# Compressed probabilities of two heads stacked on 128 rows, and one product for the bias rows of all heads

## The chip, the cores and the metric

The kernel runs on one core of a Trainium2 chip, as one launch. The metric is the device time of a run in microseconds (us). Everything is computed in 32-bit floats. TensorE is called PE in the profile, and its weight loads PEld; VectorE is DVE, ScalarE is ACT, GpSimd is POOL, and SP is the engine whose queue issues every DMA.

## What is computed

The reference is one decoder layer over 1024 tokens of width 2048: a projection `proj = h @ w_in` into 76 tiles of 128 channels, attention of 16 heads (4 groups of 4 heads, 64 channels a head), a state-space layer, gates, two branch products, an output product and a norm. Two pieces of it matter here. Scores get a bias that depends on the distance of query and key alone, through a table of 32 buckets; and each head attends, in one of three branches, to 63 compressed keys:

```python
def head_bias(dist):
    b = tbl[_t5_bucket(dist)]
    return jnp.moveaxis(b, -1, 0).reshape(G, R, *dist.shape)
...
s = jnp.einsum('bgrqd,bgnd->bgrqn', qs, kc).astype(jnp.float32)
s = s + head_bias(t[:, None] - cmp_end[None, :])
p_c = _masked_softmax(s, cmp_end[None, :] <= t[:, None])
o_c = jnp.einsum('bgrqn,bgnd->bgrqd', p_c.astype(dtype), vc)
...
o = o_c * g[..., 0:1] + o_s * g[..., 1:2] + o_w * g[..., 2:3]
```

## The kernel before, in words

**Products.** A product of accuracy near 32 bits is made of three passes of a faster type: the operand and the weights are each split into a high and a low part (`hi` by a copy on ACT, `lo` by a subtraction on DVE), and high times high, high times low and low times high are added in PSUM. `mm6` (L119 to L128) does so for the projection: 128 rows of weights, 512 tokens, six products for each of 16 slices of the 2048 channels. `dense` (L238) runs one projection tile: four units of weights of 256 KB, 24 products a unit, and a side job after each unit. `w_unit` (L104) loads a unit into one of two raw buffers and splits it into one of three pairs of buffers. Four more uses of the same scheme are the branch and output products (L454 to L464, L599 to L603).

**Order of the work.** The program is written stage by stage: the modulation (L147 to L205), the projection tiles with the state-space blocks between them (L403 to L418), the compressed keys and values (`compress`, L659), then the projection tiles of the gates with 22 early units of attention between them (L427 to L439), then 10 late units of attention with the branch products between them (L553 to L573), then the output. A scheduler that simulates the program places each engine's instructions within that, and each engine and the SP queue then runs its own list in order.

**Bias rows.** Between the modulation and the first `dense`, L336 to L351 make a table for each head. `rb` (32 buckets by 16 heads) is repeated 128 times a head into `rbx` (L345). For each head a plain 32-bit product of 32 rows (L348) gives the 384 biases by distance in all 128 partitions alike, in a PSUM bank from `bank()`; DVE adds a mask (L350, buffer `ln`), and SP stores 128 x 384 elements (192 KB) into `tz_d` in memory (L351). `bf_d` takes the mask itself, loaded as `mk` and stored again (L342, L343). Each group of attention later reads `tz_d` so that each partition is shifted by one element, as `BN` (L780).

**A unit of attention** (`Attention.unit`, L818) is one group of 4 heads and one block of 128 queries. PE makes the scores (L814), DVE adds the bias and takes the minimum, ACT takes the exponential. The probabilities lie with queries in the partitions, so `flip` (L931) transposes them on PE (L935), at most four pieces of 128 columns into one bank, and ACT and DVE split the bank into high and low (L939, L940). `values` (L954) multiplies them with the values into the unit's PSUM bank `O`, 128 partitions by 512 columns: the value tile has the high part of 64 channels and the low part of the same 64 channels side by side, so both come out above each other, and the end of the unit adds them (L1024 to L1027). For window and selected keys a piece is 128 keys by two heads, thus 128 rows and 256 columns (`weigh`, L962). For the compressed keys a head has 64 keys: `compressed_values` (L997) transposes each head's 128 x 64 block into 64 rows, and makes two products of 64 rows by 512 columns, one with the high and one with the low probabilities. `VC` (L781) is the value tile for that, 64 x 128, loaded once a group in each of the two attention stages.

Of the kernel before, what the change touches and what calls it, by code (L numbers as in the profile page):

```python
# [5 lines left out]
F32 = mybir.dt.float32  # L6
F32R = mybir.dt.float32r
# [6 lines left out]
ADD, SUB, MUL, MAX, MIN = ALU.add, ALU.subtract, ALU.mult, ALU.max, ALU.min  # L14
# [4 lines left out]
H = 16  # L19
# [31 lines left out]
def _hybrid(es, tc, A, out):  # L51
    nc = tc.nc
    V, S, P, PE = nc.vector, nc.scalar, nc.gpsimd, nc.tensor
    ld, st_ = nc.sync.dma_start, nc.sync.dma_start
    rd = nc.sync.dma_start
# [6 lines left out]
    def scratch(name, shape):  # L62
        return dp.tile(shape, F32, name=name)
# [15 lines left out]
    kcc_d = scratch("kcc_d", [128, G, 64])  # L79
    vcc_d = scratch("vcc_d", [64, G, 128])  # L80
    tz_d = [scratch(f"tz_d{g}", [4, 128, 384]) for g in range(G)]
    bf_d = scratch("bf_d", [128, 512])
    ob_d = [[scratch(f"ob_d{hf}_{i}", [2, 128, 512]) for i in range(8)] for hf in range(2)]
    oa_d = [[scratch(f"oa_d{hf}_{g}", [2, 128, 2, 512]) for g in range(G)] for hf in range(2)]
# [69 lines left out]
    for b in range(NB):  # L154
        t = xh.tile([128, T], F32, name=f"xa{b}", tag="xh"), xh.tile([128, T], F32, name=f"xb{b}", tag="xh")
# [25 lines left out]
    for k in range(0, KT, 2):  # L181
        mp = pp.tile([128, 512], F32, name="mp", tag="mp", bufs=2)
        for n in range(8):
            wa = was.pop(4 * k + n) if 4 * k + n in was else load_wa(4 * k + n)
            for i in range(2):
                r = 32 * (2 * n % 4 + i)
# [61 lines left out]
    def bank():  # L248
        return pss.tile([128, 512], F32, name="sps", tag="s")
# [86 lines left out]
    with tc.tile_pool(name="t5", bufs=1) as t5:  # L336
        rb = t5.tile([32, H], F32, name="rb")
        ld(rb, A["rel_bias"])
        oh = t5.tile([32, 384], F32, name="oh")
        ld(oh, A["onehot"][:, 384:])  # L340
        mk = t5.tile([128, 768], F32, name="mk")
        ld(mk, A["dist_mask"][0:1, :].to_broadcast([128, 768]))  # L342
        st_(bf_d, mk[:, :512])  # L343
        rbx = t5.tile([32, H, 128], F32, name="rbx")
        V.tensor_copy(rbx, rb.unsqueeze(2).to_broadcast([32, H, 128]))  # L345
        for h in range(H):
            tp = bank()
            PE.matmul(tp[:, :384], rbx[:, h], oh, start=True, stop=True)  # L348
            ln = t5.tile([128, 384], F32, name="ln", tag="ln", bufs=2)
            V.tensor_tensor(ln, tp[:, :384], mk[:, 384:], op=ADD)  # L350
            st_(tz_d[h // 4][h % 4], ln)  # L351

    def gate_steps():

# [51 lines left out]
    n = 0  # L406
# [332 lines left out]
class Attention:  # L739
# [25 lines left out]
    def group(self, g):  # L765
        V, rd, NK = self.nc.vector, self.rd, self.NK
        self.g = g

        def f(ap):
            return ap.bitcast(F32)  # L770


        if self.first == 0:
            self.window_keys(0, NK)
        self.KS = self.tl("ks", [128, NK], F32R, "k")
        rd(f(self.KS), self.k_d[0][g].rearrange("i d t -> (i d) t")[:, :NK])

        self.BN = self.tl("bn", [128, 4, 256], F32, "kv")
        t = self.tz_d[g]
        rd(self.BN, bass.AP(tensor=t.tensor, offset=t.offset + 127, ap=[[383, 128], [384 * 128, 4], [1, 256]]))  # L780
        self.VC = self.tl("vc", [64, 128], F32R, "kv")  # L781
        rd(f(self.VC), self.vcc_d[:, g])
        if self.BF is None:
            self.BF = self.tl("bf", [128, 384])
            t = self.bf_d
            rd(self.BF, bass.AP(tensor=t.tensor, offset=t.offset + 127, ap=[[511, 128], [1, 384]]))
        nb = NK // 128
        self.VS = self.tl("vs", [128, nb, 128], F32R, "kv")
        self.VW = self.tl("vw", [128, nb, 128], F32R, "kv")
        for v, t in ((self.VW, self.v_d[1][g]), (self.VS, self.v_d[0][g])):  # L790
            for hf in range(2):
                c = slice(4 * hf, min(4 * hf + 4, nb))
                rd(f(v)[:, c], t[hf][:, :c.stop - c.start])
        self.BC = self.tl("bc", [128, 4, 120 - 8 * self.first], F32, "kv")
        V.memset(self.BC[:, :, 0:48], 0.0)
        V.memset(self.BC[:, :, 63:], NEG)
        V.tensor_copy(self.BC[:, :, 48:63], self.BN[:, :, 31:256:16])
# [20 lines left out]
    def unit(self, qb):  # L818
# [4 lines left out]
        def f(ap):  # L823
            return ap.bitcast(F32)
# [106 lines left out]
        def flip(srcs, n):  # L931

            tp = self.psum("t")
            for i, x in enumerate(srcs):
                PE.transpose(tp[0:n, 128 * i:128 * i + 128], x, self.ident[:, :128])  # L935
            w = 128 * len(srcs)
            hi = self.tl("pth", [128, 512], F32R, "pt")
            lo = self.tl("ptl", [128, 512], F32R, "pt")
            S.copy(hi[0:n, :w], tp[0:n, :w])  # L939
            V.tensor_tensor(lo[0:n, :w], tp[0:n, :w], f(hi[0:n, :w]), op=SUB)  # L940
            return hi, lo
# [7 lines left out]
                compressed(h, ps[:, 64 * h:64 * h + 64])  # L949
        gt = self.gts[:, qb, 12 * g:12 * g + 12].rearrange("p (h c) -> p h c", c=3)  # L950
        nbw, nbs = nw // 128, ns // 128
        left = [2 * (nbw + nbs) + 1]

        def values(o, v, hl):  # L954
            left[0] -= 1
            for i, x in enumerate(hl):
                PE.matmul(o, v, x, start=O_new[0], stop=left[0] == 0 and i == 1)  # L957
                O_new[0] = False
# [36 lines left out]
            return r  # L995

        def compressed_values():  # L997
            values(O, self.VC, [x[0:64] for x in flip([pc[:, h] for h in range(4)], 64)])

        win = (2, window, pw, nbw, self.VW[:, qb + 1 - nbw:])  # L1000
        sel = (1, selected, pS, nbs, self.VS)
# [431 lines left out]
```

## Time and profile before

| | before |
|---|---|
| time, median of 3 runs | 3239.2 us (3238.16 to 3239.89) |
| time of the profiled execution | 3234.84 us |
| its span, first to last instruction | 3233.1 us |
| PE busy | 3162.2 us, 15603 matrix instructions |
| DVE busy | 1686.2 us |
| ACT busy | 1127.2 us |
| mean granted clock of TensorE | 0.991 |
| read from and written to memory | 331.30 MB and 98.05 MB |

The times in the rows come from the profiled execution, which took 4.4 us less than the median. "Busy" of PE is time in which a matrix instruction is in its pipeline; since they overlap, what one costs is seen from the distance of the starts, not from its own duration. The granted clock is a share of the higher of two levels, 1.2 and 2.4 GHz.

### The profile page before, as it was taken

What the parts mean: (1) busy time and instruction counts of PE and PEld (TensorE: products, weight loads), DVE (VectorE), ACT (ScalarE), POOL (GpSimd) and SP (SyncE); (2) the same over time, 40 slices, a digit from 0 to 9 for tenths busy, and PEclk for the clock granted to TensorE, in tenths of its full rate; (3) what the DMA queues carried; (4) which work ended last, traced back from release to release, by engine and by line L of the source; (5) the groups of instructions that cost most, each with busy time, mean ns of one, the idle gap of its engine ahead of it and who ended that gap; (6) DMA issues with size and microseconds to landing.
All of it is one profiled execution on the core that took longest, in us unless ns stands there. A gap on an engine that the chain in (4) does not pass through costs nothing.

```text
span 3233.1 us, 43112 instructions
## 1 busy us (share of the span) xinstructions
PE 3162.2 (98%) x15603; PEld 2538.1 (79%) x15603; DVE 1686.2 (52%) x4615; ACT 1127.2 (35%) x2327; POOL 85.5 (3%) x66
## 2 busy tenths in 40 slices
PE   7999999999999999999999999999999999999896
PEld 4467788888888888888888888887888888788784
DVE  8354678763444434334333334426777665534737
ACT  4212222222433334333433234325555443322323
POOL 0000000000000000000000000000000000000302
PEclk9999999999999999999999999999999999999998
DMA  9654524344322232222322222236668444734533
GB/s 335 236 170 147 172 94 141 103 128 119 117 92 74 77 97 88 71 64 83 97 77 74 67 84 91 76 126 202 213 207 285 142 131 147 241 114 144 166 119 138
DMA packets 286398, 432.21 MB, mean 134 GB/s; under 512 B 40324, under 2 KB 139428, under 8 KB 286184
## 3 DMA queue, kind: packets, MB, share of 16 engines
q1 hardware_dynamic: 286184, 429.45, 41.0%
q8 instruction: 123, 2.02, 0.3%
q14 instruction: 91, 0.75, 0.1%
HBM read 331.30 MB, written 98.05 MB: 133 GB/s over the span
## 4 chain that ended last, share of the span: by engine, by line
PE 93%; DVE 3%; DMA 2%; ACT 1%; issue 1%; SPq 0%; ACTq 0%; DVEq 0%
PE dps L124 17%; PE dps L125 17%; PE dps L128 17%; PE po L957 5%; PE ps L814 4%; PE pt L935 4%; PE pa L462 4%; PE pa L463 4%; PE pa L464 4%; PE e L602 2%; PE e L601 2%; PE e L603 2%; PE mp L187 2%; DVE r L595 1%; PE acc L124 1%; PE e L462 1%
## 5 line engine op out<-in xcount | busy, mean ns | idle before, releaser
L124 PE MATMUL dps<-hhi,whi 128*128 128x512 f32 x2336 | 927.8, 397 | 0.0
L125 PE MATMUL dps<-hlo,whi 128*128 128x512 f32 x2336 | 925.2, 396 | 0.0
L128 PE MATMUL dps<-hhi,wlo 128*128 128x512 f32 x2336 | 750.3, 396 | 0.0
L111 ACT CAST whi<-wraw 128x512 fp32r<-128x512 f32 x544 | 336.2, 619 | 1054.9 <-PE dps L125 622.7
L113 DVE TENSOR_TENSOR wlo<-wraw,whi 128x512 fp32r<-128x512 f32 x544 | 381.0, 701 | 600.9 <-ACT whi L111 587.8
L124 PEld LDWEIGHTS dps<-hhi,whi 128*128 128x128 f32 x2336 | 439.7, 188 | 103.8 <-issue 13.0
L125 PEld LDWEIGHTS dps<-hlo,whi 128*128 128x128 f32 x2336 | 439.8, 188 | 93.7 <-issue 7.0
L128 PEld LDWEIGHTS dps<-hhi,wlo 128*128 128x128 f32 x2336 | 433.4, 188 | 92.5 <-issue 5.7
L940 DVE TENSOR_TENSOR ptl<-pt,pth 128x512 fp32r<-128x512 f32 (+2 forms) x320 | 204.1, 646 | 269.3 <-ACT pth L939 267.6
L939 ACT CAST pth<-pt 128x512 fp32r<-128x512 f32 (+2 forms) x320 | 172.0, 552 | 456.7 <-PE pt L935 456.0
L462 PE MATMUL pa<-op,whi 128*128 128x512 f32 x528 | 210.0, 400 | 2.1 <-ACT op L449 1.7
L463 PE MATMUL pa<-op,whi 128*128 128x512 f32 x528 | 209.7, 397 | 2.5 <-DMA op<-oa_d 2.5
L464 PE MATMUL pa<-op,wlo 128*128 128x512 f32 x528 | 208.8, 396 | 0.0
L602 PE MATMUL e<-wlo,m 128*128 128x512 f32 x368 | 148.0, 402 | 9.9 <-DVE rsd L42 5.4
L603 PE MATMUL e<-whi,m 128*128 128x512 f32 x368 | 146.3, 398 | 0.0
L929 ACT ACTIVATE psl<-psl,mn 128x128 f32<-128x128 f32 (+7 forms) x128 | 99.2, 775 | 81.3 <-DVE mn L842 80.5
L601 PE MATMUL e<-whi,m 128*128 128x512 f32 x368 | 122.0, 401 | 0.6 <-ACT whi L111 0.6
L462 PEld LDWEIGHTS pa<-op,whi 128*128 128x128 f32 x528 | 99.8, 189 | 23.3 <-ACT op L449 3.3
L463 PEld LDWEIGHTS pa<-op,whi 128*128 128x128 f32 x528 | 99.6, 189 | 22.9 <-DMA op<-oa_d 2.9
L464 PEld LDWEIGHTS pa<-op,wlo 128*128 128x128 f32 x528 | 99.6, 189 | 20.1 <-issue 0.7
L904 POOL TENSOR_TENSOR near<-bn,msk 128x512 f32<-128x512 f32 x32 | 35.1, 1098 | 2662.1 <-DVE msk L900 2535.9
L883 ACT ACTIVATE pw<-pw,mn 128x640 f32<-128x640 f32 (+4 forms) x128 | 88.9, 694 | 32.4 <-DVE mn L842 31.6
(308 smaller groups left out, 4271.1 us busy)
## 6 DMA issues: line engine op xcount, KB each, us to landing
wraw<-in_w_in SPq DMA_DIRECT2D x304, 256.0 KB, 3.0
wraw<-in_w_out SPq DMA_DIRECT2D x136, 256.0 KB, 3.0
wa<-in_w_ss SPq DMA_DIRECT2D x64, 512.0 KB, 5.7
wg<-in_w_gate SPq DMA_DIRECT2D x32, 512.0 KB, 3.6
q<-q_d SPq DMA_DIRECT2D x64, 256.0 KB, 4.1
wraw<-in_w_bn SPq DMA_DIRECT2D x64, 256.0 KB, 3.1
q_d<-stg SPq DMA_DIRECT2D x32, 256.0 KB, 3.9
oa_d<-ptl SPq DMA_DIRECT2D x64, 128.0 KB, 2.2
```

Of the source, the lines that this page charges most:

```text
L111: S.copy(hi, raw)
L113: V.tensor_tensor(lo, raw, f(hi), op=SUB)
L124: PE.matmul(ps[hf], hi[:, ku], hhi[k][:, c], start=a, stop=False)
L125: PE.matmul(ps[hf], hi[:, ku], hlo[k][:, c], start=False, stop=False)
L128: PE.matmul(ps[hf], lo[:, ku], hhi[k][:, c], start=False, stop=z)
L462: PE.matmul(ps, hi[:, j], x[k][0], start=k == 0, stop=False)
L463: PE.matmul(ps, hi[:, j], x[k][1], start=False, stop=False)
L464: PE.matmul(ps, lo[:, j], x[k][0], start=False, stop=k == 7)
L601: PE.matmul(a, mk[0][:, t], hi, start=k == 0, stop=False)
L602: PE.matmul(a, mk[0][:, t], lo, start=False, stop=False)
L603: PE.matmul(a, mk[1][:, t], hi, start=False, stop=k == KT - 1)
L940: V.tensor_tensor(lo[0:n, :w], tp[0:n, :w], f(hi[0:n, :w]), op=SUB)
```

## The change

**Bias rows.** `rb` itself is the stationary operand, so one product of 32 rows gives the biases of all 16 heads in 16 partitions. DVE adds the mask once, SP stores the 16 rows in `t5_d` in memory, and sixteen DMAs then copy from memory to memory: one row of 384 elements, read 128 times, becomes the 128 x 384 table of a head in `tz_d`. `bf_d` is filled from the input in the same manner.

**Compressed values.** Two heads of a pair are transposed together, 128 x 128, so the even head lies in rows 0 to 63 and the odd head in rows 64 to 127. `VC` becomes two tiles of 128 x 128: for the even head the values stand in the upper 64 rows and zeros in the lower, for the odd head the other way round. Each parity is one product of 128 rows by 256 columns (the two pairs), high and low: four products a unit, into the columns of `O` of that parity. The zeros are set by DVE and the values loaded twice a group.

```diff
@@ -79,6 +79,7 @@
     kcc_d = scratch("kcc_d", [128, G, 64])
     vcc_d = scratch("vcc_d", [64, G, 128])
     tz_d = [scratch(f"tz_d{g}", [4, 128, 384]) for g in range(G)]
+    t5_d = scratch("t5_d", [H, 384])
     bf_d = scratch("bf_d", [128, 512])
     ob_d = [[scratch(f"ob_d{hf}_{i}", [2, 128, 512]) for i in range(8)] for hf in range(2)]
     oa_d = [[scratch(f"oa_d{hf}_{g}", [2, 128, 2, 512]) for g in range(G)] for hf in range(2)]
@@ -338,17 +339,17 @@
         ld(rb, A["rel_bias"])
         oh = t5.tile([32, 384], F32, name="oh")
         ld(oh, A["onehot"][:, 384:])
-        mk = t5.tile([128, 768], F32, name="mk")
-        ld(mk, A["dist_mask"][0:1, :].to_broadcast([128, 768]))
-        st_(bf_d, mk[:, :512])
-        rbx = t5.tile([32, H, 128], F32, name="rbx")
-        V.tensor_copy(rbx, rb.unsqueeze(2).to_broadcast([32, H, 128]))
+        mk = t5.tile([H, 384], F32, name="mk")
+        ld(mk, A["dist_mask"][0:1, 384:].to_broadcast([H, 384]))
+        tp = bank()
+        PE.matmul(tp[0:H, :384], rb, oh, start=True, stop=True)
+        ln = t5.tile([H, 384], F32, name="ln")
+        V.tensor_tensor(ln, tp[0:H, :384], mk, op=ADD)
+        st_(t5_d, ln)
+
         for h in range(H):
-            tp = bank()
-            PE.matmul(tp[:, :384], rbx[:, h], oh, start=True, stop=True)
-            ln = t5.tile([128, 384], F32, name="ln", tag="ln", bufs=2)
-            V.tensor_tensor(ln, tp[:, :384], mk[:, 384:], op=ADD)
-            st_(tz_d[h // 4][h % 4], ln)
+            st_(tz_d[h // 4][h % 4], t5_d[h:h + 1].to_broadcast([128, 384]))
+        st_(bf_d, A["dist_mask"][0:1, :512].to_broadcast([128, 512]))
 
     def gate_steps():
 
@@ -778,8 +779,11 @@
         self.BN = self.tl("bn", [128, 4, 256], F32, "kv")
         t = self.tz_d[g]
         rd(self.BN, bass.AP(tensor=t.tensor, offset=t.offset + 127, ap=[[383, 128], [384 * 128, 4], [1, 256]]))
-        self.VC = self.tl("vc", [64, 128], F32R, "kv")
-        rd(f(self.VC), self.vcc_d[:, g])
+
+        self.VC = self.tl("vc", [128, 2, 128], F32R, "kv")
+        for e in range(2):
+            V.memset(f(self.VC)[64 - 64 * e:128 - 64 * e, e], 0.0)
+            rd(f(self.VC)[64 * e:64 * e + 64, e], self.vcc_d[:, g])
         if self.BF is None:
             self.BF = self.tl("bf", [128, 384])
             t = self.bf_d
@@ -949,7 +953,7 @@
                 compressed(h, ps[:, 64 * h:64 * h + 64])
         gt = self.gts[:, qb, 12 * g:12 * g + 12].rearrange("p (h c) -> p h c", c=3)
         nbw, nbs = nw // 128, ns // 128
-        left = [2 * (nbw + nbs) + 1]
+        left = [2 * (nbw + nbs) + 2]
 
         def values(o, v, hl):
             left[0] -= 1
@@ -995,7 +999,11 @@
             return r
 
         def compressed_values():
-            values(O, self.VC, [x[0:64] for x in flip([pc[:, h] for h in range(4)], 64)])
+
+            hl = flip([pc[:, 2 * pr:2 * pr + 2].rearrange("p h n -> p (h n)") for pr in range(2)], 128)
+            Oe = O.rearrange("p (r e t) -> p r e t", r=2, e=2)
+            for e in range(2):
+                values(Oe[:, :, e], self.VC[:, e], [x[:, :256].rearrange("p (r t) -> p r t", r=2) for x in hl])
 
         win = (2, window, pw, nbw, self.VW[:, qb + 1 - nbw:])
         sel = (1, selected, pS, nbs, self.VS)
```

**Where it moves instructions.** The scheduler's order, one row an instruction or a run of alike ones; L numbers of the changed kernel are 1 higher as far as the bias rows (`mm6` is L120 to L129), and 4 to 8 higher further down (`flip` L939, `values` L961, scores L818).

PE, at the bias products (`sps<-oh,rbx`), a piece of the first `dense` in the kernel before; the first four stand in one row ahead of it, and six more follow it one at a time:

```order
L124 MATMUL dps<-hhi_1112,whi 128x512
L348 MATMUL sps<-oh,rbx 128x384 x2
L125 MATMUL dps<-hlo_1114,whi 128x512
L128 MATMUL dps<-hhi_1112,wlo 128x512 x2
L124 MATMUL dps<-hhi_1135,whi 128x512
L125 MATMUL dps<-hlo_1137,whi 128x512
L124 MATMUL dps<-hhi_1135,whi 128x512
L125 MATMUL dps<-hlo_1137,whi 128x512
L128 MATMUL dps<-hhi_1135,wlo 128x512
L348 MATMUL sps<-oh,rbx 128x384 x2
L128 MATMUL dps<-hhi_1135,wlo 128x512
```

PE, the same place in the changed kernel, from the last products of the stage ahead (`acc`):

```order
L126 MATMUL acc<-hlo_1414,whi 128x512 x2
L129 MATMUL acc<-hhi_1412,wlo 128x512 x2
L345 MATMUL sps<-oh,rb 16x384
L125 MATMUL dps<-hhi_1067,whi 128x512
L126 MATMUL dps<-hlo_1069,whi 128x512
L125 MATMUL dps<-hhi_1067,whi 128x512
L126 MATMUL dps<-hlo_1069,whi 128x512
L129 MATMUL dps<-hhi_1067,wlo 128x512 x2
```

All sixteen are one row now, and `dense` runs on behind it with no bias product between.

PE, the first unit's products with the compressed values (`po<-pth,vc` and `po<-ptl,vc`) among `dense`, before:

```order
L125 MATMUL dps<-hlo_1321,whi 128x512
L128 MATMUL dps<-hhi_1319,wlo 128x512 x2
L957 MATMUL po<-pth,vc 128x512
L814 MATMUL ps<-ks,q 128x256 x4
L957 MATMUL po<-ptl,vc 128x512
L124 MATMUL dps<-hhi_1342,whi 128x512
L125 MATMUL dps<-hlo_1344,whi 128x512
L124 MATMUL dps<-hhi_1342,whi 128x512
```

and in the changed kernel:

```order
L126 MATMUL dps<-hlo_1322,whi 128x512
L129 MATMUL dps<-hhi_1320,wlo 128x512 x2
L961 MATMUL po<-pth,vc 128x2x128
L818 MATMUL ps<-ks,q 128x256 x4
L961 MATMUL po<-ptl,vc 128x2x128
L961 MATMUL po<-pth,vc 128x2x128
L961 MATMUL po<-ptl,vc 128x2x128
L125 MATMUL dps<-hhi_1343,whi 128x512
L126 MATMUL dps<-hlo_1345,whi 128x512
L125 MATMUL dps<-hhi_1343,whi 128x512
```

Two products of 512 columns that stand apart became four of 2 x 128 columns, and three of them stand together. The transposes ahead of them (`pt<-ident,pc`) went from `64x128 x4` to `128x128 x2`.

SP, the stores of the bias tables (`tz_d<-ln`) among the loads of weights (`wraw`) and of the side job (`wg`), before:

```order
L109 DMA wraw<-in_w_in 128x512
L351 DMA tz_d_196<-ln 128x384 x2
L362 DMA wg<-in_w_gate 128x4x256 x2
L351 DMA tz_d_196<-ln 128x384 x2
L351 DMA tz_d_197<-ln 128x384 x4
L109 DMA wraw<-in_w_in 128x512
L351 DMA tz_d_198<-ln 128x384 x4
L109 DMA wraw<-in_w_in 128x512
L351 DMA tz_d_199<-ln 128x384 x4
```

and in the changed kernel, where `t_d` is `t5_d`:

```order
L110 DMA wraw<-in_w_in 128x512
L348 DMA t_d<-ln 16x384
L363 DMA wg<-in_w_gate 128x4x256 x2
L351 DMA tz_d_196<-t_d 128x384 x4
L110 DMA wraw<-in_w_in 128x512
L351 DMA tz_d_197<-t_d 128x384 x4
L351 DMA tz_d_198<-t_d 128x384 x4
L110 DMA wraw<-in_w_in 128x512
L351 DMA tz_d_199<-t_d 128x384 x4
L363 DMA wg<-in_w_gate 128x4x256
```

One small store stands ahead of the copies now, and the first load of weights behind it stands after four copies, the next after twelve.

## Rows read from the trace of the kernel before

**Rows 1.** The page: part 1 (busy), part 2 (rates), part 4 (chain by engine).

```profile
PE 3162.2 (98%) x15603; PEld 2538.1 (79%) x15603; DVE 1686.2 (52%) x4615; ACT 1127.2 (35%) x2327; POOL 85.5 (3%) x66
...
GB/s 335 236 170 147 172 94 141 103 128 119 117 92 74 77 97 88 71 64 83 97 77 74 67 84 91 76 126 202 213 207 285 142 131 147 241 114 144 166 119 138
...
PE 93%; DVE 3%; DMA 2%; ACT 1%; issue 1%; SPq 0%; ACTq 0%; DVEq 0%
```

**Rows 2.** Stretches: length; busy us PE, PEld, DVE, ACT, POOL; clock; DMA; GB/s.

```profile
200.00:250.00 50.00, 50.00 (x244) 34.01 (x245) 28.48 (x91) 7.22 (x13) 0.00 (x0) 1.00 0.49 156
...
2450.00:2500.00 50.00, 49.93 (x275) 42.26 (x274) 39.87 (x120) 28.67 (x60) 2.08 (x2) 1.00 0.96 334
```

**Rows 3.** Timeline of PE, one unit's compressed values: start us, us, instruction.

```profile
851.05 0.62 PE L128 MATMUL dps<-hhi,wlo 128*128 128x512 f32 x2
851.60 0.49 PE L957 MATMUL po<-pth,vc 64*128 64x512 f32 x1
852.02 0.74 PE L814 MATMUL ps<-ks,q 128*128 128x256 f32 x4
852.69 0.49 PE L957 MATMUL po<-ptl,vc 64*128 64x512 f32 x1
853.11 0.50 PE L124 MATMUL dps<-hhi,whi 128*128 128x512 f32 x1
853.45 0.39 PE L125 MATMUL dps<-hlo,whi 128*128 128x512 f32 x1
```

**Rows 4.** Instructions of L957: duration ns min/median/max, first and last start us, forms.

```profile
L957 PE MATMUL po<-pth,vc x32: 489/494/501, 851.6 to 2722.8; 64*128 64x512 f32 x32
```

**Rows 5.** The chain in order of time, late attention: start us, us.

```profile
2206.74 0.87 PE pt L935 x8
...
2236.99 0.84 PE po L957 x7
```

**Rows 6.** Timeline of PE round the bias products, 178 to 202 us.

```profile
178.82 4.03 PE L348 MATMUL sps<-oh,rbx 32*128 32x384 f32 x8 [1.86 <-ACT stg L214]
...
182.78 0.80 PE L124 MATMUL dps<-hhi,whi 128*128 128x512 f32 x1
...
187.20 0.62 PE L128 MATMUL dps<-hhi,wlo 128*128 128x512 f32 x2
...
188.12 0.40 PE L124 MATMUL dps<-hhi,whi 128*128 128x512 f32 x1
188.44 1.55 PE L348 MATMUL sps<-oh,rbx 32*128 32x384 f32 x4
189.92 0.50 PE L125 MATMUL dps<-hlo,whi 128*128 128x512 f32 x1
...
198.69 0.40 PE L124 MATMUL dps<-hhi,whi 128*128 128x512 f32 x1
199.02 0.91 PE L348 MATMUL sps<-oh,rbx 32*128 32x384 f32 x2
199.86 0.50 PE L125 MATMUL dps<-hlo,whi 128*128 128x512 f32 x1
200.29 0.91 PE L348 MATMUL sps<-oh,rbx 32*128 32x384 f32 x2
201.13 0.74 PE L128 MATMUL dps<-hhi,wlo 128*128 128x512 f32 x2
```

**Rows 7.** A stretch of 10 us at the bias products, columns as above.

```profile
180.00:190.00 10.00, 10.00 (x26) 5.92 (x24) 2.69 (x5) 0.58 (x1) 0.00 (x0) 0.66 1.07 333
```

**Rows 8.** Timeline of the SP queue: two loads of dense weights.

```profile
182.66 0.49 SPq L109 DMA_DIRECT2D wraw<-in_w_in  x1
...
197.07 0.33 SPq L109 DMA_DIRECT2D wraw<-in_w_in  x1
```

**Rows 9.** Instructions of L654: duration ns, first and last issue us; landing.

```profile
L654 SPq DMA_DIRECT2D gate<-gate_d x4: 650/788/877, 2752.6 to 2761.3; - x4
...
DMA to landing us min/median/max: 6.1/6.8/8.4
```

## Prediction

> **What bounds the kernel now.** I read the page first: PE is busy for 3162 of 3233 us, and PE makes 93% of the chain that ended last [rows 1]. Then the stretches of 50 us, to see whether that holds where the change acts. It does: at the bias products PE is busy for 50 of 50 us, and in the late attention for 49.93, although DVE is at 39.87 there [rows 2]. So what leaves PE's list shortens the run, and what leaves DVE's, ACT's or a queue's list does so only if PE was waiting for it. Then the timeline of PE at the two places. Matrix instructions overlap there, so I price each by the distance of the starts. Dense products follow each other at 0.23 us: four of them lie between 187.20 and 188.12 us [rows 6].
>
> **Compressed products, removed.** A 64-row product lasts 0.49 us and a dense one about 0.39, which would suggest a small difference, but the starts say more [rows 3]. Two dense products begin at 851.05, so the next was due at 851.51; the 64-row product begins at 851.60, which is 0.09 late. The second one, at 852.69, holds PE until 853.11, 0.42 us. The dense product behind it keeps PE for 0.34 us, to 853.45, in place of 0.23: another 0.11. Together 0.62 us for work of 512 columns that costs 0.23 with 128 rows. There are 32 with the high and as many with the low probabilities, the 32 that the row counts alike within 12 ns [rows 4], and in the order of before no two of the 64 stand side by side, so each pays on both sides. Removed: 64 x 0.62 = 39.7 us. The Trainium skill, TensorEngine Tiling (Array Packing), Key Properties, gives a reason: a change between the full array and 64-row tiles drains the engine. The late start and the slow first dense product agree with it.
>
> **Compressed products, added.** 128 products of 128 rows by 2 x 128 columns. The nearest rows are the products of 128 rows by 256 columns, seven of which take 0.84 us of the chain, 0.12 each [rows 5]: 128 x 0.12 = 15.4 us. What the trace does not show is an output in two pieces of 128 columns. If each piece cost as much as a transpose of 128 columns, 0.87 / 8 = 0.11 us [rows 5], a product would take 0.22, and all 28. Below 0.11 I see no row, so that the bounds are 14 and 28 us. I take 15.4, since input, weights and columns are those of the nearer row and only the output differs. Gain 24.3 us, bounds 11.5 and 25.7.
>
> **Transposes.** Four a unit become two of twice the rows of output; by the same row a transpose costs 0.11. 64 fewer: 7.0 us. ACT and DVE split 128 x 256 where they split 64 x 512, half as long a row; that is off the path while PE is busy, and I count nothing for it.
>
> **Bias products.** After 188 us three pairs of heads and six single ones stand among the dense products [rows 6]. A pair: the product at 188.12 ends its turn at 188.35, the next dense one begins at 189.92, and it costs 0.11 more as above: 1.68 us, three times 5.0. Singles come two by two with one dense product between: from 198.69 + 0.23 to 201.13 are 2.21 us, less 0.23 for the dense one, plus 0.11 for the one behind: 2.09 us, three times 6.3. Together 11.3 us, all of it removed, since the new order puts one product ahead of the first dense one and none behind it.
>
> The first four heads took 178.82 to 182.78 us. One product stays, 0.84 us by the singles (199.02 to 199.86). What this frees is worth less than 3.1 us, because of the clock: PE had waited for ACT just before [rows 6], and the stretch from 180 to 190 us had 0.66 of the clock [rows 7], that is some 7 us at the lower level. From 182.78 to 187.20 ten dense products went through, 0.44 us each. If the lower level again lasts from about 180.2 to 187.2, dense now begins at 179.7 and sends 2 and then 16 products through by 187.2 where it sent 10: 8 x 0.23 = 1.9 us. Bounds: nothing, if the first dense product waits for something else until 182.78, and 3.1 if the clock stays up. Bias products in all 13.2 us.
>
> **What goes beside.** DVE loses the wide mask additions and gets two memsets of 64 x 128 a group. A memset must wait for the last product with the old `VC`, and DVE's list waits with it; but in the changed order it stands behind the old unit's later work, so the product is long done, and I count nothing. If it were not, the splits of weights queued behind it on DVE would be late, and `dense` after them, with up to three units in hand. SP gets one more load of `VC` a group: nothing. The fill of `bf_d` moves to about 37 us, into the load of the modulation weights: 256 KB at the 335 GB/s of the first slice [rows 1] are 0.8 us at most; with the chain PE's for 93% I count nothing and keep 0.8 for the range.
>
> The copies of the bias tables matter more. SP must wait until the 16 rows have landed in memory, and the loads of weights queue behind. Before, the fifth unit's load was issued at 182.66 and the sixth's at 197.07 [rows 8]; the sixth now stands behind four copies and the seventh behind twelve. The first unit ends at about 188.6 us (18 of its 24 products by 187.2, six more at 0.23), and each further one takes 5.5, so PE reaches the seventh at about 188.6 + 5 x 5.5 = 216 us. The copies can begin at about 186, an estimate: product and addition end near 181, and the store and the two loads of the side job come first. So twelve copies have some 29 us. The nearest row is the broadcast loads of 256 KB: the last of twelve was issued at 2761.3 and landed at most 8.4 us later, some 18 us after the first at 2751.3 [rows 9]: 1.5 us each, and a copy has three quarters of that size. They are hidden with room. If that cover were gone, a late seventh unit is the next to stop PE.
>
> **Sum.** 24.3 + 7.0 + 13.2 = 44.5 us. The profiled execution took 3234.8, so 3190.3; the median of the runs lies 4.4 above it, so **3194.7 us**.
>
> **Rivals.** *The late attention gives nothing back.* Ten of the 32 units run there. For it: DVE at 39.87 of 50 us. Against: PE at 49.93 in the same stretch [rows 2]. If PE then waited for DVE and ACT instead, ten units times 0.98 us (31.3 / 32) would be lost: 3204.5.
>
> *The 0.62 us is not a matter of 64 rows*, but of the bank, or of the wait for the split that stands ahead. For it: the rows do not separate these. Against: the plain bias products of 32 rows show the same 0.1 us behind them. The products would then gain nothing, and what is left is 20.2 us: 3219.0. The Trainium skill, TensorE: Matmul & The Clock Gate, Why this matters for your kernels, speaks for this rival, as it says that a lone product of 32 rows takes the same time as one of 128. Rows 3 differ from that: 0.62 against 0.23 us.
>
> *The copies from memory to memory hold the weights back.* If they ate the whole gain of the bias products: 3207.9. The same mechanism ends **slower** from a point that can be told: beyond 2.4 us a copy each further microsecond costs 12 us, so that 44.5 us are gone at 6.1 us a copy, over four times the row's price, and at 7 us the time is 12 x 4.6 - 44.5 = 10.7 above before: 3250. For it: all 128 reads of a copy go to the same 1.5 KB, and no row shows memory to memory. Against: the broadcast loads read one row as often.
>
> **Chances.** The forecast 0.73; late attention 0.13; products without gain 0.04; copies eat the gain of the bias products 0.05; copies slower than before 0.03; something that brings it to no change 0.02. About 0.2% (6.5 us) is what a measurement of this kernel can tell from no change. Faster: 0.73 + 0.13 + 0.04 + 0.05 = 0.95; same 0.02; slower 0.03. The forecast's own range is 3186 to 3203: the first bias products and the pieces' cheaper bound, with some microseconds of waits that the new order moves (PE is not the chain for 7% of it). For 8 in 10 I add the late attention's case and some of the pieces' dearer bound: 3184 to 3209.
>
> **What would show it.** Right: the products with `vc` at 0.12 us distance, their neighbours at 0.23, one bias product of two passes near 179 us, dense products without a break from there to the side job, PE's busy time some 45 us less and its share unchanged. Wrong: a distance near 0.2 us for the products in two pieces; PE waiting for `wraw` between 200 and 230 us; new waits of PE for `ptl` or `psl` after 2190 us.

## The result and the profile after

The change takes 3201.62 us (median of four runs, 3200.14 to 3203.67) against 3238.68 before: ratio 0.9888, interval 0.9874 to 0.9902, a gain of 37.1 us. Forecast were 3194.7 us and 44.5 us; the time lies in the range, on its slow side. The profiled execution took 3203.67 us, 2 above its median, and that of before lay 4 under its own, so the two traces show only 31.2 us; the table further down is about these.

The page of the changed kernel, parts 1 and 4, answers to [rows 1]:

```profile
PE 3117.4 (97%) x15573; PEld 2537.0 (79%) x15573; DVE 1669.4 (52%) x4615; ACT 1120.7 (35%) x2327; POOL 85.2 (3%) x66
...
PE 92%; DMA 4%; DVE 3%; issue 1%; SPq 0%; ACT 0%; POOL 0%; ACTq 0%; DVEq 0%; POOLq 0%
```

PE's busy time fell by 44.8 us, as forecast, but its share fell too, and DMA has 4% of the chain instead of 2%. So the work left PE, and a part of what it freed became waiting for transfers.

The stretches of 10 us behind the one bias product (length; busy us PE, PEld, DVE, ACT, POOL; clock; DMA; GB/s) answer to [rows 7]:

```profile
180.00:190.00 10.00, 10.00 (x54) 7.02 (x54) 1.59 (x6) 1.24 (x2) 0.00 (x0) 0.99 0.93 259
190.00:200.00 10.00, 10.00 (x50) 7.65 (x49) 0.72 (x2) 0.62 (x1) 0.00 (x0) 1.00 0.97 246
200.00:210.00 10.00, 6.61 (x26) 4.36 (x25) 2.83 (x12) 1.59 (x3) 0.00 (x0) 0.70 0.57 201
```

The clock that was at 0.66 in the first of them is up, but from 200 to 210 us PE is busy for 6.61 us only, at 0.70 of the clock. The timeline of PE shows what stands there (start us, us, instruction, [idle <- releaser]):

```profile
201.49 0.40 PE L125 MATMUL dps<-hhi,whi 128*128 128x512 f32 x1
205.27 1.08 PE L366 MATMUL sps<-wg,cP 128*32 128x256 f32 x8 [3.39 <-DMA wg<-in_w_gate]
206.28 0.80 PE L126 MATMUL dps<-hlo,whi 128*128 128x512 f32 x1
206.88 0.63 PE L125 MATMUL dps<-hhi,whi 128*128 128x512 f32 x1
```

PE waits for a load of gate weights, `wg`, which the side job multiplies after a weight unit; the dense product behind the wait goes at the lower clock (0.43 us from 206.88 to the next, at 207.31, against 0.23). SP's timeline says why the load was late; it answers to [rows 8]:

```profile
179.08 0.49 SPq L348 DMA_DIRECT2D t_d<-ln  x1
179.93 1.87 SPq L363 DMA_DIRECT2D wg<-in_w_gate  x2
184.54 2.40 SPq L351 DMA_DIRECT2D tz_d<-t_d  x4
187.04 0.53 SPq L110 DMA_DIRECT2D wraw<-in_w_in  x1
187.63 6.12 SPq L351 DMA_DIRECT2D tz_d<-t_d  x8
194.03 0.35 SPq L110 DMA_DIRECT2D wraw<-in_w_in  x1
194.87 2.39 SPq L351 DMA_DIRECT2D tz_d<-t_d  x4
197.36 0.61 SPq L363 DMA_DIRECT2D wg<-in_w_gate  x1
```

One gate load had gone out at 176.77, two go out at 179.9; the fourth stands behind all sixteen copies (`t_d` is the table `t5_d`), goes out at 197.36 and lands at 205.23, 0.04 us before PE goes on. The dense weights, which I had watched, were in time.

The products with `vc` do what was forecast. First the changed kernel's instructions of L961 (duration ns, first and last start, forms; the line of [rows 4]), then PE's timeline at the first unit, as in [rows 3]:

```profile
L961 PE MATMUL po<-pth,vc x64: 274/280/365, 838.5 to 2683.8; 128*128 128x256 f32 x64
```

```profile
838.52 0.28 PE L961 MATMUL po<-pth,vc 128*128 128x256 f32 x1
838.64 0.64 PE L818 MATMUL ps<-ks,q 128*128 128x256 f32 x4
839.12 0.28 PE L961 MATMUL po<-ptl,vc 128*128 128x256 f32 x1
839.23 0.28 PE L961 MATMUL po<-pth,vc 128*128 128x256 f32 x1
839.35 0.28 PE L961 MATMUL po<-ptl,vc 128*128 128x256 f32 x1
839.47 0.40 PE L125 MATMUL dps<-hhi,whi 128*128 128x512 f32 x1
```

Starts are 0.12 us apart, and nothing is late on either side.

Where the time went, from the starts of the same instruction in the traces, minus those in the first trace of before ("dense 200" is the 200th product of `dense`; "last values" is the last product with `po`; "stage end" is the 50th product behind it; the last column is the gain of the medians):

| kernel | first bias product | dense 200 | last dense | last values | stage end | span | median |
|---|---|---|---|---|---|---|---|
| before, us | 178.8 | 247.8 | 2179.3 | 2742.4 | 2762.3 | 3233.1 | |
| before again (e9) | -0.2 | -0.2 | -0.2 | +0.6 | +0.8 | +2.3 | |
| the change | -4.1 | -12.8 | -33.5 | -36.8 | -32.3 | -31.2 | 37.1 |
| the change again (e8) | -2.6 | -11.1 | -31.8 | -35.4 | -32.4 | -31.1 | 37.8 |
| attention alone (e1) | -0.9 | -0.9 | -21.6 | -32.0 | -28.4 | -27.2 | 30.3 |
| bias alone (e2) | -2.0 | -12.4 | -12.4 | -11.1 | -9.1 | -6.5 | 11.6 |
| copies spread (e3) | -2.6 | -14.5 | -35.2 | -40.7 | -37.0 | -36.0 | 40.6 |
| 128 rows alone (e4) | -0.1 | -0.1 | -17.0 | -21.3 | -21.4 | -18.7 | 20.5 |
| bias part late (e5) | | -17.0 | -36.0 | -42.6 | -39.5 | -39.4 | 42.4 |
| four copies (e6) | -3.9 | -18.6 | -39.0 | -42.7 | -39.6 | -37.1 | 41.1 |
| mask alone (e7) | -1.1 | -1.0 | -1.0 | -0.2 | +1.6 | +2.4 | 2.2 |

### The profile page after: what moved, and what is told of

It is laid out like the page before. It is cut to its first block, busy times and chain, and to the rows that moved or that the text cites. A ratio compares the mean times of both kernels' runs of the same rounds, so it can differ in the third digit from the quotient of the medians.

```text
span 3201.9 us, 43061 instructions
## 1 busy us (share of the span) xinstructions
PE 3117.4 (97%) x15573; PEld 2537.0 (79%) x15573; DVE 1669.4 (52%) x4615; ACT 1120.7 (35%) x2327; POOL 85.2 (3%) x66
## 4 chain that ended last, share of the span: by engine, by line
PE 92%; DMA 4%; DVE 3%; issue 1%; SPq 0%; ACT 0%; POOL 0%; ACTq 0%; DVEq 0%; POOLq 0%
PE dps L125 17%; PE dps L129 17%; PE dps L126 17%; PE po L961 4%; PE ps L818 4%; PE pt L939 4%; PE pa L464 4%; PE pa L463 4%; PE pa L465 4%; PE e L603 2%; PE e L604 2%; PE e L602 2%; PE mp L188 1%; DVE r L596 1%; PE acc L125 1%; PE acc L126 1%
## 5 line engine op out<-in xcount | busy, mean ns | idle before, releaser
L129 PE MATMUL dps<-hhi,wlo 128*128 128x512 f32 x2336 | 746.5, 397 | 0.0
L129 PEld LDWEIGHTS dps<-hhi,wlo 128*128 128x128 f32 x2336 | 433.2, 188 | 89.6 <-issue 2.3
L944 DVE TENSOR_TENSOR ptl<-pt,pth 128x512 fp32r<-128x512 f32 (+1 forms) x320 | 196.3, 621 | 270.1 <-ACT pth L943 267.7
L943 ACT CAST pth<-pt 128x512 fp32r<-128x512 f32 (+1 forms) x320 | 166.1, 531 | 435.9 <-PE pt L939 432.4
L818 PE MATMUL ps<-kw,q 128*128 128x256 f32 (+4 forms) x416 | 93.1, 328 | 6.9 <-DMA kw<-k_d 5.9
```

The source lines that it names most:

```text
L129: PE.matmul(ps[hf], lo[:, ku], hhi[k][:, c], start=False, stop=z)
L818: PE.matmul(ps[:, :z - a], q[:, 4 * i + h], K[:, c0 + a:c0 + z], start=i == 0, stop=i == 1)
```

## The experiments

**One part at a time.** e1 is the kernel before with the attention part of the change alone, e2 with the bias part alone.

```diff
 e1:
+        self.VC = self.tl("vc", [128, 2, 128], F32R, "kv")
...
+            hl = flip([pc[:, 2 * pr:2 * pr + 2].rearrange("p h n -> p (h n)") for pr in range(2)], 128)
 e2:
+        PE.matmul(tp[0:H, :384], rb, oh, start=True, stop=True)
...
+            st_(tz_d[h // 4][h % 4], t5_d[h:h + 1].to_broadcast([128, 384]))
```

Expected of e1: 

> The compressed values of the change alone; the bias rows as before. PE's order up to the first bias product is that of before, so that product should start near 178.8 us again (the change: 174.7). My theory: the 22 early units give back 20.7 us between the 1000th and the last dense product, as in the change, since nothing but PE's own time bounds them; the ten late units are worth 9.8 us of PE's time, and the 3.3 that the change showed by the last product with the values is a matter of which waits the order of the day makes, so here 3 to 10. Time 3208 to 3215 us. Rival: the late attention is bound by something other than PE and gives nothing back in any order: 3218 or more. Rival: the products' gain hangs together with the bias part: less than 15 us.

Expected of e2: 

> The bias rows of the change alone; the compressed values as before. Up to the first bias product the order is that of the change, so that product should start near 174.7 us, 4.1 before the kernel before; and PE should again wait some 3.5 us near 201 us for a load of the side job's weights, with a lower clock behind. My theory: 12.8 us gained by the 1000th dense product and kept to the end, 3224 to 3228 us. Rival: the attention hides part of it or the later order gives it back: above 3230.

Measured: e1 3208.39 us (3207.63 to 3209.15, ratio 0.9908, 0.9893 to 0.9923), e2 3227.15 us (3224.17 to 3228.49, ratio 0.9964, 0.9951 to 0.9976). The gains, 30.3 and 11.6 us, add up to 41.9, 4.8 more than the change has; the intervals, some 4 to 5 us to either side of each gain, leave it open whether that is more than noise. The attention part is worth what the sum said, 24.3 + 7.0 = 31.3 us: in the traces 20.7 over the early units and 10.4 from the last dense product to the last values. The bias part gives 11.6 where 13.2 were said. Its first product starts at 176.8 us and not near 174.7 as expected, so 2.0 us of the gain lie ahead of it; the 12.4 us of the early part are kept as far as the last dense product, and 5.9 of them are gone by the end of this trace. The new wait comes with it, as PE's timeline of e2 shows:

```profile
202.00 0.40 PE L125 MATMUL dps<-hhi,whi 128*128 128x512 f32 x1
206.68 1.08 PE L366 MATMUL sps<-wg,cP 128*32 128x256 f32 x8 [4.29 <-DMA wg<-in_w_gate]
```

**Is it the 64 rows?** e4 is the kernel before with products of 128 rows that keep the 512 columns, the number 64, and the four transposes a unit: each pair of heads is transposed twice and multiplied by one value tile, which leaves out the odd heads' compressed values.

```diff
-            values(O, self.VC, [x[0:64] for x in flip([pc[:, h] for h in range(4)], 64)])
+            hl = flip([pc[:, 2 * pr:2 * pr + 2].rearrange("p h n -> p (h n)") for pr in (0, 1, 0, 1)], 128)
+            values(O, self.VC[:, 0], hl)
```

Expected: 

> As the kernel before in the bias rows. In each unit four transposes as before, but of two heads each, and two products of 512 columns as before, but with 128 rows in place of 64 (the second half of the columns repeats the first and the odd heads are left out, so the compressed branch is computed wrongly). Number of products and of columns is that of before; only the rows differ. Theory that the 0.62 us belong to 64 rows: a product now costs 0.23 us, 64 x 0.39 = 25 us less in all, of which the 22 early units give 17 and the late ones up to 8: 3213 to 3222 us. Rival, that it belongs to the bank or to the wait for the split ahead: still some 0.6 us each and 3235 to 3242 us.

Measured: 3218.25 us (3216.18 to 3219.07, ratio 0.9937, 0.9923 to 0.995). Its timeline of PE at the first unit:

```profile
851.71 0.40 PE L960 MATMUL po<-pth,vc 128*128 128x512 f32 x1
851.94 0.63 PE L817 MATMUL ps<-ks,q 128*128 128x256 f32 x4
852.41 0.40 PE L960 MATMUL po<-ptl,vc 128*128 128x512 f32 x1
852.64 0.40 PE L125 MATMUL dps<-hlo,whi 128*128 128x512 f32 x1
```

From 851.71 to 851.94 and from 852.41 to 852.64 are 0.23 us, the step of a dense product, where 64 rows cost 0.62 [rows 3]. By the distances of the starts the 64 products cost 15.1 us in place of 39.4. Bank, output columns and places in the order are those of before, the four transposes take as long as before (0.35 us a unit), and the split that stands ahead has the same columns, on twice the rows; so the rival that blamed bank or split falls: the price was that of the 64 rows among products of the full array. The Trainium skill says in TensorE: Matmul & The Clock Gate, Why this matters for your kernels, that a single product of 32 rows takes the time of one of 128. Here no product stands alone: among products of the full array one of 64 rows costs 0.39 us more (e4 against [rows 3]). The Trainium skill's drain at a change of tiling, TensorEngine Tiling (Array Packing), Key Properties, fits the 0.09 us ahead of such a product and the 0.11 behind it, though no row shows the drain itself.

**Are the copies to blame for the wait?** e3 spreads the sixteen copies over the eight steps of the state-space stage, two a step.

```diff
-        for h in range(H):
-            st_(tz_d[h // 4][h % 4], t5_d[h:h + 1].to_broadcast([128, 384]))
...
+        for h in (2 * b, 2 * b + 1):
+            st_(tz_d[h // 4][h % 4], t5_d[h:h + 1].to_broadcast([128, 384]))
```

Expected: 

> The change, but of the sixteen copies from memory to memory two are issued after each of the eight state-space blocks in place of all after the store of the bias rows. My theory: the sixteen copies in one go, 0.6 us of the SP queue each, delay the load of the side job's weights for which PE waits 3.8 us at 201 us, and the clock's lower level that follows costs some 3 more; spread out, that wait goes and the 1000th dense product comes 6 to 7 us earlier than in the change, near 469 us. Time 3193 to 3197 us. Rival: that load is late for another reason (its buffer comes free late): the wait stays and so does the time, 3200 to 3203.

Measured: 3198.12 us (3195.34 to 3205.47, ratio 0.9879, 0.9865 to 0.9892). The edit did not do what it said: the copies have nothing to wait for, and SP issues them from 188.7 to 205.5 us all the same, one to six at a time between other loads. The wait came later and was a little shorter:

```profile
209.68 0.39 PE L125 MATMUL dps<-hhi,whi 128*128 128x512 f32 x1
212.82 0.64 PE L364 MATMUL sps<-wg,cP 128*32 128x256 f32 x8 [2.75 <-DMA wg<-in_w_gate]
```

It is the wait for another load: the fourth gate load now goes out at 190.05 us, behind two copies, and PE does not wait for it; the fifth goes out at 206.03, behind the last ones, and is late in its place. The end of dense product 1000 came 1.7 us earlier than in the change, not 6 to 7, and the time lies between theory and rival. That fits the copies but does not separate them from the rest of the queue. Two more kernels do. e5 puts the whole bias part behind the state-space stage, e6 leaves it in its place with four copies and lets all groups read the first group's table.

```diff
 e5:
     sc_cm.__exit__(None, None, None)
+    with tc.tile_pool(name="t5", bufs=1) as t5:
...
     while n < n_group[0]:
 e6:
-        for h in range(H):
+        for h in range(4):
             st_(tz_d[h // 4][h % 4], t5_d[h:h + 1].to_broadcast([128, 384]))
...
-        t = self.tz_d[g]
+        t = self.tz_d[0]
```

Expected of e5: 

> The change, with the whole bias part (its three loads, the one product, the sum, the store, the sixteen copies and the mask copy) put behind the state-space stage, where SP issues the copies at some 780 to 800 us, among other transfers and with the weights in time. Theory (the sixteen copies stand ahead of the side job's first gate weights on SP's queue, PE waits 3.8 us for them at 201.5 us and runs at the lower clock behind it): no wait over 1 us at 195 to 215 us, the granted clock of 200 to 210 us at 1.0, and dense product 1000, which ended at 475.9 us in the change and 488.7 before, comes 5 to 7 us earlier than in the change, near 469 to 471 us; the end some 4 to 7 us under the change, 3195 to 3198 us. Rival (the gate weights are late there whatever stands ahead of them, because the side job starts with the first weight unit): the wait stays at 3 to 5 us, dense 1000 stays within 1.5 us of the change's, and the time is 3200 to 3204 us. Third: the copies at 790 us hold up weights there, with a wait of 3 us or more at 780 to 810 us: then the gain ends there and the time is the change's.

Expected of e6: 

> The change, with four of the sixteen memory-to-memory copies in the same place and twelve left out: all groups read the table of group 0, so that the bias rows of heads 4 to 15 are those of heads 0 to 3. The transfers that read the tables keep their size and number. Theory (it is the number of copies that delays the gate weights): SP reaches the second gate weight load some 8 us earlier than in the change (197.4 us there), near 189 us; the wait at 201.5 us goes or falls under 1 us; dense 1000 comes 4 to 6 us earlier than in the change, and the time is 3195 to 3199 us. Rival (the lost time at 200 to 215 us comes with the pause behind the one bias product and the lower clock, not with the copies): dense 1000 within 1.5 us of the change's 475.9 us, time 3200 to 3204 us.

Measured: e5 3196.21 us (3193.86 to 3199.22, ratio 0.9869, 0.9854 to 0.9884), e6 3197.49 us (3195.61 to 3200.38, ratio 0.9873, 0.9857 to 0.989). Stretches of e5, columns as above:

```profile
190.00:200.00 10.00, 10.00 (x54) 7.10 (x53) 9.14 (x42) 1.24 (x2) 0.00 (x0) 1.00 0.48 154
200.00:210.00 10.00, 10.00 (x50) 7.59 (x48) 0.99 (x3) 2.21 (x4) 0.00 (x0) 1.00 0.72 210
```

SP's timeline of e6, the four copies and the fourth gate load:

```profile
184.51 2.40 SPq L351 DMA_DIRECT2D tz_d<-t_d  x4
187.01 0.54 SPq L110 DMA_DIRECT2D wraw<-in_w_in  x1
187.60 0.42 SPq L1204 DMA_DIRECT2D U<-us_d  x1
188.07 0.42 SPq L1208 DMA_DIRECT2D B<-in_b_re  x1
188.60 0.53 SPq L363 DMA_DIRECT2D wg<-in_w_gate  x1
```

With twelve copies less the gate load goes out at 188.60 instead of 197.36 and lands at 195.41; PE begins with it at 201.78 without a wait, and the clock, 1.00 from 200 to 210 us, stays up. From the first bias product to dense product 200 the kernel gains 18.6 - 3.9 = 14.7 us on before, the change 12.8 - 4.1 = 8.7. So the twelve copies cost 6.0 us in these traces (6.2 with e8 in place of the change): 3.4 of waiting, the rest the lower clock behind it. In e5 no bias product stands there at all, and the copies go out from 681.8 to 697.1 us (I had expected 780 to 800), among dense products that run on without a wait over 0.2 us. Dense product 1000 ended 4.3 us earlier in e5 than in the change, at 471.6 us, short of the 5 to 7 expected, and 5.8 earlier in e6, at 470.1, within its 4 to 6.

By its median e5 also is the fastest kernel of the study: its four runs, 3193.86 to 3199.22 us, lie below all eight runs of the change (3199.33 to 3203.76), about 5 us or 0.15 to 0.17% by the medians, for a block of code that stands elsewhere. That is under the 0.2% that the prediction gave as what a measurement can tell, and the intervals of the ratios overlap, so by the times alone the step from the change to e5 stays unproven; the vanished wait is what the traces show.

**The early lead.** The first bias product of the change begins 4.1 us earlier, a gain for which the sum had no term. e7 is the kernel before with the mask edits alone, which move PE's order in the first 180 us.

```diff
-        mk = t5.tile([128, 768], F32, name="mk")
-        ld(mk, A["dist_mask"][0:1, :].to_broadcast([128, 768]))
-        st_(bf_d, mk[:, :512])
+        mk = t5.tile([128, 384], F32, name="mk")
+        ld(mk, A["dist_mask"][0:1, 384:].to_broadcast([128, 384]))
+        st_(bf_d, A["dist_mask"][0:1, :512].to_broadcast([128, 512]))
...
```

Expected: 

> The kernel before, with the mask edits of the change alone: the mask row is loaded 384 wide, and bf_d is written from memory to memory. The sixteen products, sums and stores stay. These edits move the order on PE in the first 180 us: the 32-column products stand in 49 runs instead of 51 (48 in the change). Theory (the 2 to 4 us that the change and its parts gained before the first bias product come from this order, since a run of two 32-column products takes as long as a run of four, near 1 us): the first bias product starts 1 to 3 us earlier than the 178.8 us of before, the lead stays to the end, 3236 to 3238 us. Rival (the early lead is scatter between executions, or comes from the product that replaces the sixteen): first bias product within 0.9 us of 178.8, time 3238 to 3240 us.

Measured: 3236.61 us (3230.80 to 3238.99, ratio 0.9992, 0.9983 to 1.0001), no difference that can be told; the first bias product is 1.1 us earlier, where the theory began and the rival all but ended. This run decides nothing. The table says a little more. Three traces with the order of before begin at -0.9 to -0.1 (before again, e1, e4). The five with the change's order, of 48 runs of 32-column products, lie at -2.0 to -4.1. The two groups don't overlap, but two executions of the same kernel differ by 1.5 us (e8 against the change), and e7 lies between them. So a lead of 2 to 4 us comes with the changed order, which nobody meant to alter; that the order is its cause is likely but not shown.

**The late stages.** The change lost 4.5 us between the last values and the stage end, and 6.5 of the late attention's 9.8 are missing. e8 is the change and e9 the kernel before, both unaltered, for second traces.

Expected of e8: 

> The change itself, unaltered, for a second trace. In its first trace it lost 5.2 us against before between the 400th and 600th product of the first output stage (a wait of 4.4 us at 2297 us for a load of the state-space results) and 4.5 us at the end of the attention (a wait of 6.2 us for the last reloaded attention rows, then the lower clock). Theory (both come with the order of the changed kernel): both waits stand in this trace again, 3.5 to 5.5 us and 5 to 7 us long, and the products of the late attention give back 2 to 5 us of the 9.8 us worked out. Rival (they are scatter between executions; the profiled execution of before was 4 us under its median and that of the change 2 us over): one of the two waits shrinks under 2.5 us. Under both, the wait of 3 to 4.5 us at 201 us for the gate weights is there again, and dense product 1000 within 1.5 us of 475.7 us.

Expected of e9: 

> The kernel before, unaltered, for a second trace. Theory (the places of the waits are fixed by the order): the wait near 2325 us stays under 2 us, that behind the last attention product near 3 us, and every milestone lies within 1.5 us of the first trace, but that trace was some 4 us faster than the median, so the end may lie 2 to 6 us later, by waits that a comparison of the two traces will place. Rival (scatter in the late stages): waits of 3 to 6 us at 2300 to 2330 us or behind the last attention product, as in the change.

Measured: e8 3200.88 us (3199.33 to 3203.76, ratio 0.988, 0.9863 to 0.9897), e9 3237.14 us in its one run. In e8 the wait for the gate weights is there again (3.65 us, until 207.0), and dense product 1000 lies 1.7 us later than in the change, just outside the 1.5 expected. The wait at the stage end is there again too (5.53 us). First the change's timeline of PE, then that of before:

```profile
2714.13 0.40 PE L463 MATMUL e<-op,whi 128*128 128x512 f32 x1
2720.28 0.79 PE L464 MATMUL pa<-op,whi 128*128 128x512 f32 x1 [5.75 <-DMA op<-oa_d]
2720.87 0.63 PE L465 MATMUL pa<-op,wlo 128*128 128x512 f32 x1
```

```profile
2752.40 0.39 PE L462 MATMUL e<-op,whi 128*128 128x512 f32 x1
2755.27 0.50 PE L463 MATMUL pa<-op,whi 128*128 128x512 f32 x1 [2.48 <-DMA op<-oa_d]
2755.61 0.40 PE L464 MATMUL pa<-op,wlo 128*128 128x512 f32 x1
```

The last attention rows go to memory and come back. Before they let PE go on 12.9 us after the last values (13.1 in e9), in the change 14.6 (14.4 in e8; 13.6 to 14.7 in e1, e3, e5 and e6, which all have the attention part; 12.8 to 13.3 in e2, e4 and e7). And behind the longer wait PE goes on at the lower clock (0.43 us from 2720.87 to the next), while in before steps of 0.43 us stood ahead of the wait, from 2745.06 to 2749.32, in time that PE would have spent waiting anyway. The longer return comes with the attention part in every trace that has it, so the theory holds for the wait. It does not hold for the clock, whose lower level moves from trace to trace: e8 has 6 steps of 0.43 us behind its wait where the change has 14, and e2 and e7, with the attention of before, have 8 and 7 there.

Nor does it hold for the wait at 2297 us, in which ACT waits for a load of the state-space results (`stg<-y_d`, 4.40 us) that stands on SP's queue among loads of queries and values. In the change, then the last of these rows in e8:

```profile
2295.95 0.40 PE L465 MATMUL pa<-op,wlo 128*128 128x512 f32 x1
2297.20 0.50 PE L818 MATMUL ps<-kw,q 128*128 128x256 f32 x2 [0.85 <-DVE mn L846]
2301.84 0.80 PE L463 MATMUL pa<-op,whi 128*128 128x512 f32 x1 [4.13 <-ACT op L450]
```

```profile
2302.45 0.80 PE L463 MATMUL pa<-op,whi 128*128 128x512 f32 x1 [1.87 <-ACT op L450]
```

In e8 the wait is 1.87 us instead of 4.13, under the 2.5 that the rival named; the wait at the entry of the stage, for a load of keys, is 7.82 instead of 5.93 (4.84 before). There the place stays and the length is scatter. In all, PE is idle between the last dense product and the last values for 8.1 us before, 13.6 in the change, 12.7 in e8 and 9.1 in e1, so that 5.5 of the change's missing 6.5 us are waits. e9 came out as its theory said as far as the stage end: its waits there are of 1.6 us at most near 2335 and of 2.9 behind the last values, and no column of the table moves by more than 0.8 before the span, which is 2.3 longer. What the ten late units give back differs accordingly: 3.3 and 3.5 us in the two traces of the change, 3.7 in e6, 5.4 in e3, 6.6 in e5, 10.4 in e1.

## Why the prediction was right, and where its terms were off

- **Bound, and products removed and added:** right. The 64 products of 64 rows cost 39.4 us by the distances of all their starts (39.7 said), the 128 in two pieces 15.2 (15.4 said). The dearer bound for two pieces, 28, did not come about. e4 shows that the rows were the reason.
- **Transposes:** right. The 128 took 11.8 us, start to start, and the 64 that stay take 4.9: 6.9 us less, 7.0 said.
- **Early units:** 22 units gave 33.5 - 12.8 = 20.7 us, 0.94 each, where 0.98 was said.
- **First bias products, 1.9 us said:** more. I let the lower clock last to 187.2 us whatever stood ahead of it. It lies behind PE's pause and moved forward with it: in the change dense products step by 0.43 us from 176.7 to 180.1, then by 0.23. Nor is it sure to come: in e2, behind the same pause of 1.86 us, they step by 0.23 from the second one on, and the granted clock is 1.00 from 174 to 200 us. The bias part without the wait (e6) gives 14.7 us, which is 11.3 plus about the upper bound of 3.1.
- **"They are hidden with room":** this step failed. The price of a copy was not the reason: the last of the sixteen was issued 12.2 us after the first, under the 1.5 us each that were said, and a copy lands 5.7 us after its issue (median of sixteen). The cover was named wrongly. I timed the copies against the seventh load of dense weights, needed at 216 us; the first thing behind them that PE needs is the fourth gate load, due at 201.8 (by e6). The rival "copies hold the weights back" had the mechanism but counted the wrong cover: 6.0 us lost, not the 13.2 that it took.
- **Late attention:** between forecast and rival. The rival blamed DVE, which is not it: in the change PE is busy for 49.98 us and DVE for 39.02 from 2400 to 2450 us, and for 48.84 and 33.66 from 2450 to 2500. PE's longer waits are for transfers, at the stage's entry and at the state-space results. That about two thirds of the gain are missing in the change and nothing in e1 I can describe but not forecast.
- **Stage end:** not in the sum; 4.5 us in the traces, of which 1.8 are the later return of the rows, and the rest mostly the lower clock behind the wait instead of ahead of it, which e8 shows less of (3.0 us lost in all).
- **Early stage, no term in the sum:** 2 to 4 us of gain, likely by an order that moved.

So in the first traces: 4.1 + 8.7 + 20.7 + 3.3 - 4.5 = 32.3, less 1.1 behind the stage end, is the 31.2 us of the spans. The medians show 37.1, since the profiled execution of before was a quick one of its kind: in e9 the span is 2.3 us longer.

That the time lies in the stated range is in part luck. The losses that the sum left out, 6.0 us by the copies, 6.5 in the late attention and 4.5 at the stage end, were made up in part by the early lead, which it left out as well; without these 2.0 to 4.1 us the time would be 3203.6 to 3205.7, an estimate from the traces, and outside the 3203.

What stays open: why one execution returns 3 us in the late attention and another kernel's 10, and how much of the early lead is the order.

## What to carry to other kernels

When a queue gets new entries, list everything behind them in that queue and the time at which PE needs each, not only the stream one has in mind; here a side job's load, not the weights, was first. A product on half of the rows among full ones costs far more than its columns say, so two half-height operands stacked into one full product pay even when half of the values are zeros. Work that isn't needed for 600 us can stand where nothing is short: with the bias part moved, the wait was gone.

## What the runs showed of the hardware that was not expected

A copy from memory to memory that reads one row 128 times (192 KB) lands 5.7 us after its issue, where the same table from the chip's own buffers landed in 2.2 us; SP's entry takes 0.59 us in place of 0.32. The rows of L351, the change and before (duration ns min/median/max, first and last issue; landing):

```profile
L351 SPq DMA_DIRECT2D tz_d<-t_d x16: 469/592/878, 184.5 to 196.7; - x16
DMA to landing us min/median/max: 4.0/5.7/7.3
```

```profile
L351 SPq DMA_DIRECT2D tz_d<-ln x16: 319/320/512, 183.2 to 209.7; - x16
DMA to landing us min/median/max: 1.8/2.2/5.3
```

In e5 sixteen of them went out in 15.3 us, and from 660 to 860 us PE waited for nothing over 0.2 us.

The products of 32 columns in the first stage go to four places of 32 output partitions in turn. PE's timeline of the change shows a run of two (four records) and a run of four (eight records), each with its successor:

```profile
113.55 1.05 PE L188 MATMUL mp<-wa,cP 128*32 128x512 f32 x4
114.53 0.50 PE L129 MATMUL acc<-hhi,wlo 128*128 128x512 f32 x1
...
116.67 1.07 PE L188 MATMUL mp<-wa,cP 128*32 128x512 f32 x8
117.67 0.51 PE L129 MATMUL acc<-hhi,wlo 128*128 128x512 f32 x1
```

From start to start the two take 0.98 us and the four 1.00. The Trainium skill, TensorE: Matmul & The Clock Gate, Why this matters for your kernels, says that products on different column groups run at the same time, and the rows agree: up to four of them cost what one run costs (six take 1.84 us), so that two or three runs fewer would be worth 2 to 3 us, an estimate; e7, with two fewer, began 1.1 us earlier.
